# One branch for crowded experts at the end of a two-block transformer kernel, in place of one branch in each expert layer

## The chip, the cores and the metric

One core of one Trainium2 chip runs the whole program. The metric is device time in microseconds (us) of one execution, from three runs of a kernel; beside them one further execution is recorded by the hardware profiler. The program has five instruction streams: TensorE (PE in the profile, with its weight loads as PEld), VectorE (DVE), ScalarE (ACT), GpSimd (POOL) and SyncE (SP). All weight loads are issued from SP's queue.

## What is computed

A sequence of 256 tokens of width 1024 goes through one block (gated feed-forward, a mix of dilated attention and a recurrence, a second feed-forward) and then through a second block with two mixing layers, each followed by a layer of 16 experts. The change touches the expert layers, from here on called layer 0 and layer 1. Cut to what matters, the reference is:

```python
def grouped_moe(x, router_w, router_bias, w1, w3, w2):      # x: 256 tokens, 16 experts of width 512
    ...
    _, idx = lax.top_k(jnp.where(in_group, sel, -jnp.inf), TOP_K)     # 2 experts of one group of 4
    ...
    h = jax.nn.silu(jnp.einsum('td,edf->etf', xt, w1)) * jnp.einsum('td,edf->etf', xt, w3)
    h = h * gates.T[:, :, None].astype(h.dtype)
    y = jnp.einsum('etf,efd->td', h, w2)

for i in range(DEPTH_2):                                     # the second block, 2 layers
    mix = ...                                                # s5 + pooling (i = 0), stick-breaking attention (i = 1)
    x = layer_norm(DEEPNORM_ALPHA * x + mix, ln_mix_g[i], ln_mix_b[i])
    ple = (p[i] @ ple_w_proj[i]) * jax.nn.sigmoid(x @ ple_w_gate[i])
    ffn = grouped_moe(x, router_w, router_bias, moe_w1[i], moe_w3[i], moe_w2[i])
    x = layer_norm(DEEPNORM_ALPHA * x + ffn + ple, ln_ffn_g[i], ln_ffn_b[i])
```

## The kernel before, in words

The kernel gives every expert room for CAP = 64 tokens. `router` (line 1181) chooses the experts, numbers the tokens of each one, and counts: `cn` is the largest number of tokens that any expert got, `ci` the same as an integer. An expert with more than 64 tokens is crowded; the tokens beyond 64 are then computed by `overflow` (line 1504), which sends all 256 tokens through all 16 experts.

`moe_layer` (line 1277) runs the experts in eight pairs, p = 0 to 7. For each pair TensorE does, in a written order (each instruction is chained to the one before by `pinned`, line 337): `combine` of the pair before (tiles `early` for p below 3, `comb` from 3 on), `hidden_T` (tile `ehT`, four transposes) and `slots_T` (tile `ohTp`), the first up-projection of the next pair (tile `h`), the down-projection of this pair (tile `ey`), the gate chunks of the embedding (tile `gacc`, for p up to 3), and the second up-projection of the next pair (tile `h` again; the trace shows its result multiplied on DVE as `es`). An up-projection reads eight weight tiles of 512 KB, a down-projection eight. Two up-projections and one down-projection make 24 tiles a pair.

At p = 4, ahead of everything else of that pair, each layer holds its branch (lines 1460 to 1464):

```python
            if p == 4:
                del cur["pin"]
                v = nc.values_load(ci[0:1, 0:1], min_val=0, max_val=T)
                with tc.If(v > CAP):
                    overflow(i, x, nh, nl, late, row)
                cur["pin"] = None
```

Each of the five engines loads the count into a register (TENSOR_LOAD, line 1461), compares and branches (COMPARE_BRANCH, line 1462), and, where the body is left out, adds to its semaphores what the body would have added (EVENT_SEMAPHORE, line 1462) before it goes on. SP has eight of these, one for each DMA semaphore. Right after the branch comes `residual` (line 1428): it adds the two halves of the layer's transposed input (`whole_h`, `whole_l`) on DVE into four tiles `yT`, transposes them back on TensorE (tile `yn`, 16 transposes of 128x128) and adds the result to the accumulators `acc`. After that stands `combine` for pair 3.

Weights come through class `Stream` (line 251): a list `specs` of all loads in the order of their use, a ring of 11 slots of 512 KB, from line 1652 on 13 more, and at the start of each expert layer some slots lent by other pools. `next` (line 286) hands out the next tile and issues the loads that fit. In SP's queue a load waits until the tile that had its slot has been read, and until the load eight places ahead of it has landed (eight DMA semaphores in turn). The scheduler of the framework orders each engine's instructions within a stretch without branches; the branch of each layer is the end of one such stretch, and nothing moves over it.

`layer_norm_out` (line 1151) ends the program: SP issues four output transfers, waits on all semaphores and the engines meet (line 1749).

Of the kernel before, what the change touches and what calls it, by code (L numbers as in the profile page):

```python
# [15 lines left out]
P = 128  # L16
# [33 lines left out]
def transformer_kernel(ctx: ExitStack, tc: tile.TileContext, A, out, stop=None):  # L50
# [10 lines left out]
    psum = ctx.enter_context(tc.tile_pool(name="ps", bufs=4, space=bass.MemoryType.PSUM))  # L61
    pacc = ctx.enter_context(tc.tile_pool(name="pa", bufs=4, space=bass.MemoryType.PSUM))
# [176 lines left out]

    moe_specs(0)  # L240
# [10 lines left out]
    class Stream:  # L251
# [16 lines left out]
        def ahead(self, n):  # L268
            while self.n < min(len(specs), self.pos + n):
                ap = specs[self.n]  # L270
                t = self.slot([ap.shape[1], ap.shape[2]], f"w{self.n}")
                self.loads.append(nc.sync.dma_start(t, ap))
                self.tiles.append(t)
                self.n += 1

# [45 lines left out]
    def after(i, j):  # L321

        tc.add_manual_dep(i.ins, j.ins.name, mybir.DependencyInfo(
            mybir.DependencyClass.NoSync, mybir.DependencyReason.DATA), reason="order")
# [771 lines left out]
    def layer_norm_T(x, before, row, eps, then=None):  # L1096
# [23 lines left out]
        for i in range(2):  # L1120
            halves = before(i)
            r, m, _ = ln_stats(halves, eps)
            cur["z"] = S.activation(x[i][:, :512], halves[0], AF.Identity, scale=r, bias=m)
            cur["zv"] = V.tensor_scalar(x[i][:, 512:], halves[1], r, m, op0=OP.mult, op1=OP.add)
# [56 lines left out]
    def router(p, parts):  # L1181
# [45 lines left out]
        cn = SM([1], name="cn")  # L1227
        V.tensor_reduce(cn, pk[:, 2, :], axis=AX.X, op=OP.max)
        ci = spool.tile([P, 1], I32, tag="ci", name="ci", bufs=2)
        V.tensor_copy(ci, cn)  # L1230
# [6 lines left out]
        late = SM([2, NE], name="late")  # L1237
        V.tensor_scalar(late, rk, float(CAP), None, op0=OP.is_ge)
        V.scalar_tensor_tensor(late, late, 1.0 / ALPHA, sc, op0=OP.mult, op1=OP.mult)
        return oh, rk, sc, late, ci  # L1240
# [36 lines left out]
    def moe_layer(i, x, before, row, eps, next_gains):  # L1277
# [32 lines left out]
        def then(t, qs):  # L1310
# [6 lines left out]
            elif t == 1:  # L1317
# [8 lines left out]
                G.tensor_tensor(nl[1], x[1], fb(nh[1]), op=OP.subtract)  # L1326
            elif t == 2:
                routed.extend(router(lg, parts))
                W.lend(LEND)
                gather(0, routed[0])  # L1330
                W.lend([H, H])
                W.lend([X,XH]*2, 18)

        xT = layer_norm_T(x, before, row, eps, then)
        oh, rk, sc, late, ci = routed
# [92 lines left out]
        def residual():  # L1428

            for kk in range(2):  # L1430
                yT = [Q([2, T], name="yT") for _ in range(2)]
                for n in range(2):
                    c = slice(2 * n, 2 * n + 2)
                    V.tensor_tensor(yT[n], fb(whole_h[kk])[:, c], fb(whole_l[kk])[:, c], op=OP.add)  # L1434
                for t in range(2):
                    pn = PT([4, P], name="yn")
                    for k in range(4):
                        pinned(PE.transpose(pn[:, k, :], yT[k // 2][:, k % 2, t * P:(t + 1) * P], ident))  # L1438
# [19 lines left out]
        for p in range(8):  # L1458
            if p == 4:
                del cur["pin"]  # L1460
                v = nc.values_load(ci[0:1, 0:1], min_val=0, max_val=T)
                with tc.If(v > CAP):
                    overflow(i, x, nh, nl, late, row)
                cur["pin"] = None
# [9 lines left out]
            if p == last + 1:  # L1474
                residual()
# [18 lines left out]
            if p == last:  # L1494
                embedding()
            if p < 7:
                h3 = PT([512], name="h3")
                up(p + 1, h3)
                s = hidden(h1, h3)
        combine(7, y, o)  # L1500
# [3 lines left out]
    def overflow(i, x, nh, nl, late, row):  # L1504
# [5 lines left out]
        for k in range(8):  # L1510
            p = PT([2, P], name="ofp")
            for t in range(2):
                PE.transpose(p[:, t, :], xf[t][:, k * P:(k + 1) * P], ident)
# [139 lines left out]
    eps = (1e-5, 1e-5 / ALPHA ** 2)  # L1653
    f = moe_layer(0, xt, f, 0, eps[0], (2, 2))
    f = stick(xt, f, 2, eps[1])
    f = moe_layer(1, xt, f, 4, eps[0], (6, 2))
    layer_norm_out(f, eps[1])

# [94 lines left out]
```

## Time and profile before

| | us |
|---|---|
| median of three runs | 1308.74 |
| the three runs | 1304.94, 1308.74, 1309.45 |
| the profiled execution, device time | 1304.89 |
| its span, first to last instruction | 1302.7 |
| TensorE busy in the span | 1241.5 (95%) |
| mean granted TensorE clock | 0.972 of full |

The span is what the views of the trace measure; the device time of the same execution is 2.2 us longer. Layer 0 lies between about 629 and 893 us of the span, layer 1 between about 1023 us and the end. An instruction that ends in "q" in a row (DVEq, SPq) is one of the engine's sequencer: it branches, waits or issues, and does not count as busy. In the trace an up-projection has 32 records of `h`, two for each matmul of the program.

### The profile page before, as it was taken

What the parts mean: (1) busy time and instruction counts of PE and PEld (TensorE: products, weight loads), DVE (VectorE), ACT (ScalarE), POOL (GpSimd) and SP (SyncE); (2) the same over time, 40 slices, a digit from 0 to 9 for tenths busy, and PEclk for the clock granted to TensorE, in tenths of its full rate; (3) what the DMA queues carried; (4) which work ended last, traced back from release to release, by engine and by line L of the source; (5) the groups of instructions that cost most, each with busy time, mean ns of one, the idle gap of its engine ahead of it and who ended that gap; (6) DMA issues with size and microseconds to landing.
All of it is one profiled execution on the core that took longest, in us unless ns stands there. A gap on an engine that the chain in (4) does not pass through costs nothing. (4 is left out here: it accounts for less than half of the span.)

```text
span 1302.7 us, 19644 instructions
## 1 busy us (share of the span) xinstructions
PE 1241.5 (95%) x7726; PEld 906.6 (70%) x7726; DVE 607.7 (47%) x975; ACT 514.9 (40%) x774; POOL 269.3 (21%) x318
## 2 busy tenths in 40 slices
PE   8999999999999999998999997997999999997996
PEld 7999997887898999897635453445988734454433
DVE  6445548886664645477512123115755514114113
ACT  5444445575444554435421131114677422122111
POOL 4000001002499547213101220002311101220001
PEclk9999999999898999999999998998999899998998
DMA  9765565435454556536899997999835698998995
GB/s 342 232 188 184 181 191 178 131 130 169 138 179 128 176 152 199 165 128 229 325 395 384 386 385 276 395 398 369 329 112 180 218 373 302 383 389 311 358 393 216
DMA packets 175273, 335.36 MB, mean 257 GB/s; under 512 B 10337, under 2 KB 72305, under 8 KB 175170
## 3 DMA queue, kind: packets, MB, share of 16 engines
q1 hardware_dynamic: 173696, 330.34, 71.8%
q0 software_dynamic: 896, 2.98, 0.6%
q8 instruction: 64, 1.05, 0.3%
q10 hardware_dynamic: 578, 0.67, 0.2%
q14 instruction: 39, 0.32, 0.1%
HBM read 332.91 MB, written 1.05 MB: 256 GB/s over the span
## 5 line engine op out<-in xcount | busy, mean ns | idle before, releaser
L316 DVE TENSOR_TENSOR wlo<-w,whi 128x1024 fp32r<-128x1024 f32 x200 | 266.2, 1338 | 208.5 <-ACT whi L301 205.8
L301 ACT ACTIVATE whi<-w 128x1024 fp32r<-128x1024 f32 x234 | 246.4, 1059 | 247.3 <-PE hT L346 118.8
L350 PE MATMUL h<-w,xg 128*64 128x512 f32 x1024 | 225.6, 594 | 0.5
L345 PE MATMUL hT<-xTh,whi 128*128 128x256 f32 x704 | 202.1, 287 | 0.1
L346 PE MATMUL hT<-xTl,whi 128*128 128x256 f32 x704 | 201.3, 286 | 0.4 <-DVE xTl L334 0.3
L347 PE MATMUL hT<-xTh,wlo 128*128 128x256 f32 x704 | 200.8, 286 | 0.0
L350 PEld LDWEIGHTS h<-w,xg 128*64 128x64 f32 x1024 | 72.3, 137 | 137.8 <-issue 132.1
L345 PEld LDWEIGHTS hT<-xTh,whi 128*128 128x128 f32 x704 | 137.3, 195 | 1.5 <-ACT xTh L332 0.5
L346 PEld LDWEIGHTS hT<-xTl,whi 128*128 128x128 f32 x704 | 137.1, 195 | 1.4 <-DVE xTl L334 0.8
L347 PEld LDWEIGHTS hT<-xTh,wlo 128*128 128x128 f32 x704 | 136.9, 195 | 0.0
L350 PE MATMUL ey<-w,ehTs 128*64 128x512 f32 x512 | 114.2, 593 | 0.4
L335 DVE SCALAR_TENSOR_TENSOR yl<-ey,sgate,yh 128x512 fp32r<-128x512 f32 x32 | 24.0, 749 | 180.1 <-ACT yh L332 179.0
L332 ACT ACTIVATE yh<-ey,sgate 128x512 fp32r<-128x512 f32 x32 | 22.0, 688 | 167.6 <-PE ey L350 127.3
L350 PEld LDWEIGHTS ey<-w,ehTs 128*64 128x64 f32 x512 | 38.6, 137 | 70.8 <-issue 62.8
L316 POOL TENSOR_TENSOR wlo<-w,whi 128x1024 fp32r<-128x1024 f32 x16 | 37.7, 2382 | 222.2 <-ACT whi L301 142.4
L345 PE MATMUL tr<-xTh,whi 128*128 128x256 f32 x256 | 73.9, 289 | 0.4 <-ACT xTh L332 0.4
L346 PE MATMUL tr<-xTl,whi 128*128 128x256 f32 x256 | 73.2, 286 | 0.3 <-DVE xTl L334 0.3
L347 PE MATMUL tr<-xTh,wlo 128*128 128x256 f32 x256 | 72.6, 284 | 0.0
L346 PE MATMUL yacc<-wlo,hh 128*128 128x512 f32 x176 | 68.7, 391 | 0.0
L345 PE MATMUL yacc<-whi,hh 128*128 128x512 f32 x176 | 68.7, 390 | 0.0
L347 PE MATMUL yacc<-whi,hl 128*128 128x512 f32 x176 | 68.6, 390 | 0.0
L357 POOL TENSOR_TENSOR brs<-rp,cm 128x1 f32<-128x1 f32 x8 | 4.4, 550 | 299.3 <-DVE rp L356 297.4
(444 smaller groups left out, 2138.1 us busy)
## 6 DMA issues: line engine op xcount, KB each, us to landing
w<-in_moe_w SPq DMA_DIRECT2D x384, 512.0 KB, 10.2
w<-in_ffn_w SPq DMA_DIRECT2D x132, 512.0 KB, 4.3
w<-in_w_in SPq DMA_DIRECT2D x28, 512.0 KB, 3.9
w<-in_sb_qkv SPq DMA_DIRECT2D x24, 512.0 KB, 10.5
w<-in_ple_gate SPq DMA_DIRECT2D x16, 512.0 KB, 9.0
w<-in_w_out SPq DMA_DIRECT2D x8, 512.0 KB, 3.2
w<-in_ab_w_in SPq DMA_DIRECT2D x8, 512.0 KB, 4.4
w<-in_ab_w_out SPq DMA_DIRECT2D x8, 512.0 KB, 4.1
```

What stands on the lines that cost most here:

```text
L301: a = S.activation(hi, t, AF.Copy)
L316: i = eng.tensor_tensor(lo, t, fb(hi), op=OP.subtract)
L332: cur["act"] = S.activation(hi, src, AF.Copy if isinstance(scale, float) else AF.Identity, scale=scale)
L335: return V.scalar_tensor_tensor(lo, src, scale, fb(hi), op0=OP.mult, op1=OP.subtract)
L345: pinned(PE.matmul(o, lh, rh, start=start, stop=False))
L346: pinned(PE.matmul(o, lh, rl, start=False, stop=False))
L347: pinned(PE.matmul(o, ll, rh, start=False, stop=stop))
L350: pinned(PE.matmul(o, l, r, start=start, stop=stop, **kw))
L357: cur["pow"] = G.tensor_tensor(o, t, cm05[:, :n], op=OP.pow)
```

## The change

- Both branches inside the layers go, and with them the calls of `overflow` on the path that is always run. `late` (the weights of the tokens beyond 64) is no longer computed there.
- The count of layer 1's router is the maximum of both layers' counts; only then it is made an integer.
- `residual` is issued right after the second up-projection of pair 4, in the body of p = 3, and its sum on DVE is made ahead of `embedding`, as two tiles `whole` of 128x1024 instead of four `yT` of 128x512.
- Two transfers of 512 KB are added in layer 0: the layer's input goes from SBUF to two tiles `kept` in DRAM.
- At the end of the program one branch stands behind `layer_norm_out`. Its body reads `kept` back, sets the weight stream back to the first load of layer 0, and runs layer 0, the attention, layer 1 and the output again, with `overflow` called in both layers.

```diff
...
+    dpool = ctx.enter_context(tc.tile_pool(name="dram", bufs=1, space=bass.MemoryType.DRAM))
...
+    base = len(specs)
     moe_specs(0)
...
+        def back(self, n):
+
+            self.n = self.pos = n
+            del self.tiles[n:]
+            self.lent = {}
+            self.ahead(self.depth())
...
-        for i in range(2):
+        for i in range(2 if before else 0):
             halves = before(i)
...
-        cn = SM([1], name="cn")
+
+        cn = spool.tile([P, 1], F32, tag="cn", name="cn", bufs=2)
         V.tensor_reduce(cn, pk[:, 2, :], axis=AX.X, op=OP.max)
-        ci = spool.tile([P, 1], I32, tag="ci", name="ci", bufs=2)
-        V.tensor_copy(ci, cn)
+        if cur.get("cn") is not None:
+            V.tensor_tensor(cn, cn, cur["cn"], op=OP.max)
+        cur["cn"] = cn
...
-        late = SM([2, NE], name="late")
-        V.tensor_scalar(late, rk, float(CAP), None, op0=OP.is_ge)
-        V.scalar_tensor_tensor(late, late, 1.0 / ALPHA, sc, op0=OP.mult, op1=OP.mult)
-        return oh, rk, sc, late, ci
+        late = None
+        if crowded:
+            late = SM([2, NE], name="late")
+            V.tensor_scalar(late, rk, float(CAP), None, op0=OP.is_ge)
+            V.scalar_tensor_tensor(late, late, 1.0 / ALPHA, sc, op0=OP.mult, op1=OP.mult)
+        return oh, rk, sc, late
...
                 G.tensor_tensor(nl[1], x[1], fb(nh[1]), op=OP.subtract)
+                if i == 0 and not crowded:
+                    for u in range(2):
+                        nc.sync.dma_start(kept[u], x[u])
...
             for kk in range(2):
-                yT = [Q([2, T], name="yT") for _ in range(2)]
-                for n in range(2):
-                    c = slice(2 * n, 2 * n + 2)
-                    V.tensor_tensor(yT[n], fb(whole_h[kk])[:, c], fb(whole_l[kk])[:, c], op=OP.add)
                 for t in range(2):
                     pn = PT([4, P], name="yn")
                     for k in range(4):
-                        pinned(PE.transpose(pn[:, k, :], yT[k // 2][:, k % 2, t * P:(t + 1) * P], ident))
+                        pinned(PE.transpose(pn[:, k, :], whole[kk][:, k, t * P:(t + 1) * P], ident))
...
-            if p == 4:
-                del cur["pin"]
-                v = nc.values_load(ci[0:1, 0:1], min_val=0, max_val=T)
-                with tc.If(v > CAP):
-                    overflow(i, x, nh, nl, late, row)
-                cur["pin"] = None
+            if p == 4 and crowded:
+                overflow(i, x, nh, nl, late, row)
...
             if p == last + 1:
-                residual()
                 comb = [[PA([512], name="comb") for _ in range(2)] for _ in range(2)]
...
             if p == last:
+                whole = [X([4, T], name="whole") for _ in range(2)]
+                for kk in range(2):
+                    V.tensor_tensor(whole[kk], fb(whole_h[kk]), fb(whole_l[kk]), op=OP.add)
                 embedding()
             if p < 7:
                 h3 = PT([512], name="h3")
                 up(p + 1, h3)
                 s = hidden(h1, h3)
+                if p == last:
+                    residual()
...
+    kept = [dpool.tile([P, D], F32, tag=f"kept{u}", name=f"kept{u}") for u in range(2)]
     f = moe_layer(0, xt, f, 0, eps[0], (2, 2))
     f = stick(xt, f, 2, eps[1])
     f = moe_layer(1, xt, f, 4, eps[0], (6, 2))
+    ci = spool.tile([P, 1], I32, tag="ci", name="ci", bufs=1)
+    V.tensor_copy(ci, cur["cn"])
+    v = nc.values_load(ci[0:1, 0:1], min_val=0, max_val=T)
     layer_norm_out(f, eps[1])
+    with tc.If(v > CAP):
...
+        W.back(base)
+        x = [H([D], name="again") for _ in range(2)]
+        for u in range(2):
+            nc.sync.dma_start(x[u], kept[u])
+        f = moe_layer(0, x, None, 0, eps[0], (2, 2), crowded=True)
+        f = stick(x, f, 2, eps[1])
+        f = moe_layer(1, x, f, 4, eps[0], (6, 2), crowded=True)
+        layer_norm_out(f, eps[1])
```

`last` is 3. Where the change puts these instructions shows in the order of the built programs. The first place is TensorE at the branch of layer 0: `h_` is the second up-projection of pair 4, `ofp` and `ofh` belong to the body. Before:

```order
4105 L350 MATMUL h_7666<-w_7532,xg 64x512
4106 L1461 TENSOR_LOAD ci
4107 L1462 COMPARE_AND_BRANCH
4108 L1513 MATMUL ofp<-identr,of 128x128 x16
...
4253 L1462 UNCONDITIONAL_BRANCH x2
4254 L1438 MATMUL yn<-identr,yT 128x128 x16
4255 L350 MATMUL comb<-yh,ohT 128x512
```

And with the change:

```order
4105 L361 MATMUL h_7671<-w_7533,xg 64x512
4106 L1452 MATMUL yn<-identr,whole 128x128 x16
4107 L361 MATMUL comb<-yh,ohT 128x512
4108 L361 MATMUL comb<-yl,ohT 128x512
```

The 16 transposes and the eight `comb` stand where they stood; only the load of the count and the branch between them and `h` are gone. Layer 1 has the same.

The second place is DVE at the same point of layer 0 with the change (`es` is the product of the up-projections, `pg` the embedding's gate):

```order
546 L1269 TENSOR_SCALAR sgate<-ohTp 64x1 x2
547 L1506 TENSOR_TENSOR whole<-xTh,xTl 128x1024
548 L346 SCALAR_TENSOR_TENSOR yl<-ey,sgate,yh 128x512 x2
549 L1506 TENSOR_TENSOR whole<-xTh,xTl 128x1024
550 L1443 TENSOR_TENSOR pg<-pg,pro 128x512 x2
551 L1444 TENSOR_TENSOR acc<-acc,pg 128x512 x2
552 L1443 TENSOR_TENSOR pg<-pg,pro 128x512 x2
553 L1444 TENSOR_TENSOR acc<-acc,pg 128x512 x2
554 L1368 TENSOR_TENSOR es<-es,h_7671 128x512
555 L1454 TENSOR_TENSOR acc<-acc,yn 128x512 x4
```

Before, two `yT` stood ahead of `es` and two more between the additions of `yn`; now both sums are made ahead of the embedding.

The third place is SP at the start of layer 0 with the change, and at the end of the program:

```order
213 L274 DMA w_6752<-in_moe_w 128x2x512
214 L1344 DMA kept_6558<-x_87 128x1024
215 L274 DMA w_6754<-in_moe_w 128x1024
216 L1344 DMA kept_6559<-x_88 128x1024
217 L274 DMA w_6756<-in_moe_w 128x1024
...
221 L274 DMA w_6596<-in_moe_w 128x2x512
222 L274 DMA w_6764<-in_moe_w 128x1024
223 L274 DMA w_6766<-in_moe_w 128x1024
...
634 L1179 DMA out<-o 128x832
635 L1676 COMPARE_AND_BRANCH
```

The two copies stand between weight loads; the load in row 221 (its slot comes free with the tile `pro`) had stood two loads later. SP's branch stands behind the last output transfer, and each other engine's branch behind its last instruction; the body that they pass over has 5183 instructions on TensorE, 920 on DVE, 643 on ACT, 131 on POOL and 1560 on SP.

## Rows read from the trace of the kernel before

**Rows 1.** The page: the span.

```profile
span 1302.7 us, 19644 instructions
```

**Rows 2.** PE around layer 0's branch: start us, us, operation, [idle before <-releaser].

```profile
781.26 7.09 PE L350 MATMUL h<-w,xg 128*64 128x512 f32 x32
795.07 1.94 PE L1438 MATMUL yn<-identr,yT 128*128 128x128 f32 x8 [6.72 <-DVEq L1462]
...
799.94 0.78 PE L350 MATMUL comb<-yh,ohT 128*128 128x512 f32 x1
...
804.50 7.09 PE L350 MATMUL h<-w,xg 128*64 128x512 f32 x32
```

**Rows 3.** The same around layer 1's branch.

```profile
1186.47 0.60 PE L350 MATMUL h<-w,xg 128*64 128x512 f32 x2
1193.69 1.94 PE L1438 MATMUL yn<-identr,yT 128*128 128x128 f32 x8 [6.62 <-DVEq L1462]
...
1203.61 2.79 PE L350 MATMUL h<-w,xg 128*64 128x512 f32 x12
```

**Rows 4.** The same one pair later in layer 0, where no branch stands.

```profile
829.19 0.40 PE L350 MATMUL comb<-yh,ohT 128*128 128x512 f32 x1
...
831.03 0.60 PE L1356 MATMUL ehT<-identr,es 128*128 128x128 f32 x4
831.47 0.38 PE L1246 MATMUL ohTp<-identr,oh 128*128 128x128 f32 x2
...
832.14 2.37 PE L350 MATMUL h<-w,xg 128*64 128x512 f32 x10
```

**Rows 5.** Layer 0's branch by engine: ns min/median/max, first and last start us.

```profile
L1462 ACTq COMPARE_BRANCH  x1: 45/45/45, 783.1 to 783.1; - x1
L1462 ACTq EVENT_SEMAPHORE  x1: 17/17/17, 784.6 to 784.6; - x1
L1462 DVEq COMPARE_BRANCH  x1: 72/72/72, 789.2 to 789.2; - x1
L1462 DVEq EVENT_SEMAPHORE  x1: 21/21/21, 794.9 to 794.9; - x1
```

**Rows 6.** SP's longest wait of layer 0's stretch; SP's branch in layer 1.

```profile
SPq L1462 <- SPq L1462: 9.4, 1, 9.4
L1462 SPq EVENT_SEMAPHORE  x8: 17/17/17, 1171.1 to 1174.2; - x8
L1462 SPq COMPARE_BRANCH  x1: 50/50/50, 1165.7 to 1165.7; - x1
```

**Rows 7.** By stretch: us, busy PE PEld DVE ACT POOL, clock, DMA share, GB/s.

```profile
790.00:820.00 30.00, 23.86 (x106) 12.04 (x108) 8.04 (x13) 4.81 (x7) 0.00 (x0) 0.83 0.74 264
820.00:886.00 66.00, 65.90 (x331) 30.26 (x329) 8.85 (x20) 8.80 (x16) 0.00 (x0) 1.00 1.04 397
1165.00:1223.00 58.00, 49.90 (x226) 24.38 (x224) 17.18 (x27) 11.74 (x16) 0.97 (x1) 0.91 0.87 324
1223.00:1285.00 62.00, 61.90 (x312) 29.06 (x310) 8.19 (x17) 8.80 (x16) 0.00 (x0) 1.00 1.03 394
```

**Rows 8.** A wait at the end of layer 1; PE there, pair 7's down-projection.

```profile
PEld ey L350 <- DMA w<-in_moe_w: 0.8, 2, 0.5
1281.04 7.78 PE L350 MATMUL ey<-w,ehTs 128*64 128x512 f32 x32
```

**Rows 9.** DVE ahead of layer 0's branch.

```profile
784.86 1.29 DVE L1434 TENSOR_TENSOR yT<-xTh,xTl 128x512 f32<-128x512 f32 x2
```

**Rows 10.** ACT where layer 0's input is finished; SP's longest wait there.

```profile
632.42 0.83 ACT L1123 ACTIVATE x<-x,brs 128x512 f32<-128x512 f32 x1
SPq L272 <- PE pro L1268: 10.2, 2, 10.0
```

**Rows 11.** The end: SP's last transfer and its semaphore instructions.

```profile
1299.17 0.33 SPq L1168 DMA_DIRECT2D out<-o  x1
L1749 SPq EVENT_SEMAPHORE  x14: 17/28/28, 1299.6 to 1302.7; - x14
```

More of the change, by code (lines that the diff above doesn't have):

```diff
@@ L321, in after @@
     def after(i, j):
+        if j is None:
+            return
         tc.add_manual_dep(i.ins, j.ins.name, mybir.DependencyInfo(
@@ L1179, in onehot, with router @@
         return oh
-    def router(p, parts):
+    def router(p, parts, crowded):
         sc = SM([2, NE], name="score")
@@ L1275, in ple_projection, with moe_layer @@
         return [part(t, j) for t in range(2) for j in range(2)]
-    def moe_layer(i, x, before, row, eps, next_gains):
+    def moe_layer(i, x, before, row, eps, next_gains, crowded=False):
         pro = [M([D], name="pro") for _ in range(2)]
@@ L1326, in then @@
                 G.tensor_tensor(nl[1], x[1], fb(nh[1]), op=OP.subtract)
+                if i == 0 and not crowded:
+                    for u in range(2):
+                        nc.sync.dma_start(kept[u], x[u])
             elif t == 2:
-                routed.extend(router(lg, parts))
+                routed.extend(router(lg, parts, crowded))
                 W.lend(LEND)
@@ L1334, in moe_layer @@
         xT = layer_norm_T(x, before, row, eps, then)
-        oh, rk, sc, late, ci = routed
+        oh, rk, sc, late = routed
         def up(p, h, chunks=range(4)):
@@ L1512, in overflow @@
             for t in range(2):
-                PE.transpose(p[:, t, :], xf[t][:, k * P:(k + 1) * P], ident)
+                pinned(PE.transpose(p[:, t, :], xf[t][:, k * P:(k + 1) * P], ident))
             S.activation(xT[k // 4][:, k % 4, :], p.rearrange("p a b -> p (a b)"), AF.Identity,
@@ L1656, in transformer_kernel @@
     f = moe_layer(1, xt, f, 4, eps[0], (6, 2))
+    ci = spool.tile([P, 1], I32, tag="ci", name="ci", bufs=1)
+    V.tensor_copy(ci, cur["cn"])
+    v = nc.values_load(ci[0:1, 0:1], min_val=0, max_val=T)
     layer_norm_out(f, eps[1])
+    with tc.If(v > CAP):
+        for n in [n for n in cur if n != "both"]:
+            del cur[n]
+        cur.update({n: None for n in ("z", "zv", "hold")})
+        W.back(base)
[6 more added lines that the diff above has]
+        layer_norm_out(f, eps[1])
 def _constants():
```

## The prediction

> **What bounds the kernel now.** The span is 1302.7 us [rows 1]. I read TensorE's timeline first, at the two places where a branch stands. In layer 0 the second up-projection of pair 4 ends at 781.26 + 7.09 = 788.35; nothing runs on TensorE for 6.72 us, until an instruction of the branch on DVE lets it go; then come 16 transposes, the eight `comb` from 799.94 on, and the next up-projection only at 804.50 [rows 2]. From up-projection to up-projection that is 16.15 us. In layer 1 it goes from 1187.07 (1186.47 + 0.60) to 1203.61, 16.54 us [rows 3]. One pair later, without a branch and without transposes, the same `comb`, `ehT` and `ohTp` take 832.14 - 829.19 = 2.95 us, and four transposes 831.47 - 831.03 = 0.44 [rows 4]. These two places are the only wide gaps that TensorE has in the two layers.
>
> Why the gap is that long is told by the sequencers' rows. DVE's COMPARE_BRANCH takes 72 ns at 789.2, but its next instruction comes at 794.9, 5.7 us later [rows 5]; TensorE's first transpose waits for just that one. SP needs longer still: 9.4 us in layer 0, and in layer 1 5.4 us (1165.7 to 1171.1) to the first of its eight semaphore instructions [rows 6]. While SP stands there, no weights are requested.
>
> So the third view is the traffic by stretch. After layer 0's branch the DMA engines move 397 GB/s until the layer's end; in the 30 us around the gap only 264 [rows 7]. The missing part is (397 - 264) / 397 x 30 = 10.1 us of transfer. Around layer 1's branch it is (394 - 324) / 394 x 58 = 10.3 us [rows 7]. This matters since the weights are as scarce as TensorE: at the end of layer 1 TensorE waits for loads, and the last down-projection takes 7.78 us [rows 8] where an up-projection of as many records takes 7.09 [rows 2].
>
> **The change part by part.** *Both branches go.* What is left for TensorE between the up-projections is 16 transposes, at the pace of rows 4 16 / 4 x 0.44 = 1.76 us (an estimate, at full clock), and the 2.95 us of rows 4: 4.71. Freed are 16.15 - 4.71 = 11.44 us in layer 0 and 16.54 - 4.71 = 11.83 in layer 1, 23.3 in all. Part of it is the clock: the granted clock is 0.83 and 0.91 of full in the stretches around the branches and 1.00 in those behind them [rows 7], because TensorE fell to its lower level when it stood idle. The transposes' own needs are met: their sums are made ahead of the embedding, three of the four `yn` tiles take banks that were read long before, and the fourth follows `es`, which is done while the first twelve transposes run.
>
> *What is late next* are the weights. TensorE would arrive 11.4 and 11.8 us earlier at the end of the layers, but at their ends it waits for loads already, so it can gain there only what the loads gain. They can gain what they lost, 10.1 and 10.3 us: SP is no longer held, and the slots come free earlier since TensorE reads earlier. So I count 20.4 us and not 23.3. Ends for this term: nothing from below (the loads come no earlier at all), 23.3 from above. I take 20.4 since the queue's standstill is a row of its own and no load is missing a slot because of anything that stays.
>
> *The sums* `whole` cover the same columns as four `yT` (two of them take 1.29 us [rows 9]), so they cost DVE the same 2.6 us a layer; they move ahead of the embedding, where DVE waits for the gate chunks. The second has to wait for a slot that a gate chunk's low half leaves. Cost 0; without that cover at most 2.6 a layer, a bound that I don't count. The two `late` instructions and the copy of the count, all small, leave the router in layer 0; in layer 1 a maximum comes in. Cost 0, they stand behind what TensorE waits for.
>
> *The two copies to DRAM* are 0.52 MB each, 1.3 us apiece at 397 GB/s, 2.6 in all. The second waits in SP's queue until layer 0's input is finished on ACT at 632.42 + 0.83 = 633.25 [rows 10], and holds all loads behind it. But SP stands still there anyway, 10.0 us for the tile `pro` [rows 10], and the load that waits for `pro` now stands two loads earlier. I take 0, because the layer's first tiles are requested far ahead and the queue has several short stops in the pairs that follow; 2.6 is the upper end.
>
> *The branch at the end.* SP's last transfer is issued at 1299.17 + 0.33 = 1299.5, its closing semaphores run from 1299.6 to 1302.7 [rows 11]. Now a jump lies between. For its price the nearest rows are SP's own: 5.4 and 9.4 us [rows 6]. The other engines' jumps start with their last instruction, ahead of SP's last transfer, so SP's decides. Behind it come the eight semaphore instructions and the closing ones, without the wait for the last transfer, which has landed by then: between 0 and the 3.1 us of rows 11; I take 2.2, since the meeting of the engines stays as it is. The end is then 1299.5 + 5.4 + 2.2 = 1307.1 to 1299.5 + 9.4 + 2.2 = 1311.1, that is 4.4 to 8.4 us more. I take the middle, 6.4.
>
> Advanced Engine Details and Errata in the Trainium skill, section Control Flow Timing, puts a compare-and-branch at about 108 ns. The instruction alone agrees (45 and 72 ns in rows 5), the time until the engine's next one does not; by the page's figure the end would cost 0.1 us for the jump and the sum would be a gain of 20 us.
>
> **The sum** is -20.4 + 6.4 = -14.0 us. The profiled execution took 1304.89, so 1290.9. The median of the runs shown, 1308.74, lies 3.85 above it; of the four executions two are at 1304.9 and two at 1308.7 to 1309.5. I add half of the distance, 1.9: 1292.8.
>
> **The rivals.** *A short jump at the end.* ACT passed its branch in 1.5 us (783.1 to 784.6 [rows 5]), over a short body and with work of its own to wait for; and at the end no weights are in flight. With 1.5 the end is 1299.5 + 1.5 + 2.2 = 1303.2, 0.5 more than before, and the sum -19.9: 1286.9. Against it: 5.4 and 5.7 us came on two engines and in both layers, nearly alike, which looks like a fixed delay and not like traffic. The page's figure of 108 ns points this way.
>
> *Jumps that queue.* SP's 9.4 us came 1.9 us behind DVE's branch, its 5.4 with none close ahead; were the difference, 4.0, the price of each engine ahead, three (ACT, POOL, DVE) would make it 5.4 + 12 = 17.4, the end 16.4 later, and the sum -4.0: 1302.8, about no change. Against it: DVE's own 5.7 came behind TensorE's branch and was not longer. Runtime: NRT & Kernel Launch in the Trainium skill, section Instruction fetch mechanics, says that a branch past the two pages held has to fetch its target by DMA; over the large body at the end that would hold for ACT and POOL too.
>
> *Half of the loads' time comes back.* If slots and not SP's standstill held the loads, perhaps half of the 20.4 is gained: -10.2 + 6.4 = -3.8, 1303.0, no change.
>
> *Slower: the weights set the end and come no earlier.* TensorE then waits in pairs 5 to 7 for what it gained, both layers end where they ended, and the new end is paid on top: +6.4, 1313.2, with the upper price 1315. The place is the last two pairs of each layer; it turns slower than before when less than 6.4 of the 20.4 us come back. For it: the loads' wait in rows 8. Against it: in the 30 us around layer 0's branch a third of the traffic is missing, and what held it is removed.
>
> *The branch at the end is taken.* Then two layers and the attention run again. Both branches were passed over before, and the count is the larger of the same two, so I give it next to nothing.
>
> **How the numbers follow.** No change is within 0.5%, 6.5 us, about what a measurement of this kernel can tell. The forecast has 0.68, the short jump 0.13, half of the loads' time 0.07, queuing jumps 0.06, the slower case 0.05, the taken branch 0.01. Faster is the forecast and the short jump, 0.81; the same 0.13; slower 0.06. The range goes down to the short jump at the profiled execution's level (1304.89 - 19.9 = 1285.0, less one) and up to the forecast with its worst ends at the median's level: 1308.74 - 20.4 + 8.4 + 2.6 = 1299.3, and a little more for loads that come back in part: 1284 to 1301.
>
> **What would show it.** Right: between the up-projections around the 16 `yn` TensorE has no idle row, the clock stays at 1.00, the stretch takes about 4.7 us; the traffic does not fall below 380 GB/s there; the last down-projection of each layer is longer than 7.78 and waits for loads by one to three us in pairs 6 and 7. At the end SP shows a COMPARE_BRANCH and 5 to 9 us until its next instruction. Wrong: a wait of `yn` for DVE, a traffic gap that stays, waits of pair 0 or 1 for weights behind `kept`, or an end that comes within 2 us of the last transfer's landing, or more than 10 after it.

## The result, and the profile after

The changed kernel took 1289.65 us (median of four runs, 1284.18 to 1291.71), the kernel before 1308.38 (four runs); the ratio is 0.9867, with a 95% interval from 0.9844 to 0.9890. The profiled execution took 1288.41 us, 16.5 less than that of before (1304.89); the prediction had 14.0 less. The medians lie 18.7 us apart here, and 15.4 and 13.2 in two later measurements of the same two kernels (given below beside other runs); the prediction's 1292.8 was 15.9 below its median. The page's span:

```profile
span 1286.7 us, 19601 instructions
```

TensorE's timeline of the changed kernel around the two places where the branches stood (start us, us, operation):

```profile
781.07 7.09 PE L361 MATMUL h<-w,xg 128*64 128x512 f32 x32
788.08 1.97 PE L1452 MATMUL yn<-identr,whole 128*128 128x128 f32 x16
789.80 0.48 PE L361 MATMUL comb<-yh,ohT 128*128 128x512 f32 x1
...
792.83 7.09 PE L361 MATMUL h<-w,xg 128*64 128x512 f32 x32
...
1172.18 7.09 PE L361 MATMUL h<-w,xg 128*64 128x512 f32 x32
1179.20 1.97 PE L1452 MATMUL yn<-identr,whole 128*128 128x128 f32 x16
...
1183.94 7.09 PE L361 MATMUL h<-w,xg 128*64 128x512 f32 x32
```

They answer to [rows 2, 3]. From the transposes to the next up-projection it is 4.75 and 4.74 us, with no idle row in either place. The traffic and the clock in the stretches that answer to [rows 7] (us, busy PE PEld DVE ACT POOL, clock, DMA share, GB/s):

```profile
784.00:812.00 28.00, 28.00 (x144) 12.00 (x142) 8.58 (x15) 4.96 (x8) 0.00 (x0) 1.00 1.05 392
812.00:878.00 66.00, 65.33 (x318) 30.02 (x316) 8.23 (x18) 9.57 (x18) 0.00 (x0) 1.00 1.04 396
1158.00:1215.00 57.00, 57.00 (x292) 29.42 (x290) 18.72 (x31) 14.71 (x22) 0.66 (x1) 1.00 1.04 395
1215.00:1271.00 56.00, 55.64 (x257) 23.08 (x254) 5.75 (x11) 6.79 (x12) 0.00 (x0) 1.00 0.96 367
```

The holes of 264 and 324 GB/s are gone, and the clock is at full speed throughout. What is given back shows at the end of each layer, in TensorE's timeline of the last up- and down-projection:

```profile
858.05 4.79 PE L361 MATMUL h<-w,xg 128*64 128x512 f32 x18
863.12 2.42 PE L361 MATMUL h<-w,xg 128*64 128x512 f32 x8 [0.28 <-DMA w<-in_moe_w]
865.82 1.93 PE L361 MATMUL h<-w,xg 128*64 128x512 f32 x6 [0.28 <-DMA w<-in_moe_w]
...
872.78 7.79 PE L361 MATMUL ey<-w,ehTs 128*64 128x512 f32 x32
...
1249.16 6.28 PE L361 MATMUL h<-w,xg 128*64 128x512 f32 x26
1255.69 1.93 PE L361 MATMUL h<-w,xg 128*64 128x512 f32 x6 [0.26 <-DMA w<-in_moe_w]
```

Only small idle pieces are marked, but the last up-projection takes 865.82 + 1.93 - 858.05 = 9.70 us in layer 0 and 8.46 in layer 1, where one that waits for nothing takes 7.09. Most of the rest stands with the weight loads ahead of the matmuls (PEld, 857 to 868 us):

```profile
PEld h L361 <- DMA w<-in_moe_w: 3.7, 6, 1.2
```

To see where the 16.0 us of span went, the program is cut at landmarks. A *stretch* runs, in each layer, from the start of pair 4's second up-projection (781.07 and 1172.18 above) to the first `comb` behind the layer's last down-projection. All in us, from the timelines; *next* is the time from the stretch's start to the next up-projection:

| kernel | start | layer 0: next, stretch | between | layer 1: next, stretch | last matmul to the span's end |
|---|---|---|---|---|---|
| before | 781.26 | 23.24, 108.19 | 290.53 | 23.63, 108.76 | 10.84 |
| after | 781.07 | 11.76, 99.44 | 291.68 | 11.76, 98.19 | 13.20 |
| difference | -0.2 | -8.75 | +1.15 | -10.57 | +2.4 |

So the two stretches gave 19.3 us, the part between them took 1.15 back, and the new end 2.4. The end of the changed kernel, in the rows of the branch's line (ns min/median/max, first and last start us) and in SP's waits from 1270 us on (us, times, longest):

```profile
L1676 SPq EVENT_SEMAPHORE  x8: 17/17/17, 1284.5 to 1285.0; - x8
L1676 PEldq COMPARE_BRANCH  x1: 3620/3620/3620, 1273.1 to 1273.1; - x1
L1676 POOLq COMPARE_BRANCH  x1: 53/53/53, 1280.0 to 1280.0; - x1
L1676 DVEq COMPARE_BRANCH  x1: 76/76/76, 1280.2 to 1280.2; - x1
L1676 POOLq EVENT_SEMAPHORE  x1: 17/17/17, 1280.5 to 1280.5; - x1
L1676 SPq COMPARE_BRANCH  x1: 45/45/45, 1281.2 to 1281.2; - x1
L1676 DVEq EVENT_SEMAPHORE  x1: 21/21/21, 1283.2 to 1283.2; - x1
```

```profile
SPq L1676 <- SPq L1676: 3.3, 1, 3.3
```

A *jump* is the time from an engine's COMPARE_BRANCH to its next instruction. SP's takes 3.3 us (1281.2 to 1284.5), not 5.4 or 9.4 as in [rows 6], TensorE's 3.6, DVE's 3.0 and POOL's 0.5.

### The profile page after: what moved, and what is told of

Read it like the earlier page. It is cut to its first block, busy times and chain, and to the rows that moved or that the text cites. A ratio compares the mean times of both kernels' runs of the same rounds, so it can differ in the third digit from the quotient of the medians.

```text
span 1286.7 us, 19601 instructions
## 1 busy us (share of the span) xinstructions
PE 1237.8 (96%) x7726; PEld 901.8 (70%) x7726; DVE 606.5 (47%) x967; ACT 514.2 (40%) x774; POOL 270.0 (21%) x318
## 4 chain that ended last, share of the span: by engine, by line
PE 64%; issue 14%; POOL 7%; DMA 6%; DVE 5%; ACT 3%; ACTq 0%; POOLq 0%; DVEq 0%; SPq 0%
PE h L361 14%; PE ey L361 7%; DMA w<-in_moe_w 5%; PE xgp L361 3%; PE hT L356 2%; PE hT L357 2%; PE hT L358 2%; PE tr L357 2%; PE tr L356 2%; PE tr L358 2%; PE oacc L358 2%; PE oacc L356 2%; PE nat L356 2%; PE nat L357 2%; PE nat L358 2%
## 5 line engine op out<-in xcount | busy, mean ns | idle before, releaser
L361 PE MATMUL h<-w,xg 128*64 128x512 f32 x1024 | 228.8, 595 | 1.3 <-DMA w<-in_moe_w 0.8
L1368 DVE TENSOR_TENSOR es<-es,h 128x512 f32<-128x512 f32 x16 | 11.0, 687 | 119.0 <-PE h L361 105.6
## 6 DMA issues: line engine op xcount, KB each, us to landing
w<-in_moe_w SPq DMA_DIRECT2D x384, 512.0 KB, 10.3
w<-in_sb_qkv SPq DMA_DIRECT2D x24, 512.0 KB, 10.3
```

Of the source, the lines that this page charges most:

```text
L361: pinned(PE.matmul(o, l, r, start=start, stop=stop, **kw))
L1368: V.tensor_tensor(s, s, h3, op=OP.mult)
```

## The experiments

The question is not whether the branches cost what they seemed to, but by what: by holding SP's queue, as the prediction has it, or by holding TensorE, which then frees no slots. SP's waits bear on both. In the 40 us of layer 1 around the place, before and then after:

```profile
SPq L272 <- PE h L350: 14.0, 4, 11.6
```

```profile
SPq L274 <- PE h L361: 9.9, 8, 3.7
```

Behind its own jump, SP waited 11.6 us in one piece for the up-projection that TensorE began only after the gap. In layer 0 its jump, 9.4 us, fell into the gap itself, and its longest wait for an up-projection behind that was 4.6. The first two experiments separate the two holds. All are edits of the changed kernel, with no branch in the layers.

### pe_hold: TensorE held, SP free

```diff
-            V.tensor_tensor(s, s, h3, op=OP.mult)
+            cur["es"] = V.tensor_tensor(s, s, h3, op=OP.mult)
...
-                for kk in range(2):
-                    V.tensor_tensor(whole[kk], fb(whole_h[kk]), fb(whole_l[kk]), op=OP.add)
+                V.tensor_tensor(whole[1], fb(whole_h[1]), fb(whole_l[1]), op=OP.add)
                 embedding()
...
                 if p == last:
+                    for _ in range(5):
+                        j = V.tensor_tensor(whole[0], fb(whole_h[0]), fb(whole_l[0]), op=OP.add)
+                        after(j, cur["es"])
                     residual()
```

> The changed kernel with one of the two sums written five times, after the product es, so that TensorE has to stand still ahead of its 16 transposes in both layers while SP is free: es ends at 788.99 us in the changed kernel, five sums of 1.23 us end at 795.1, and TensorE idles for about 7.0 us per layer (it did for 6.7 with the branch). Theory SLOTS (the loads' lost time is TensorE's: slots come free only when it reads): in the changed kernel SP waits for a slot from 791.63 to 794.79 us; now until about 801.8, the first tile lands about 4 us later than in the changed kernel or more, and each layer ends 4 to 7 us later: 1298 to 1304 us. Theory QUEUE (the loads lost SP's own standstill, as the prediction has it): no more than 1 us per layer, 1290 to 1292 us.

1303.24 us, ratio 0.9989 (0.9975 to 1.0003): nearly all of the gain is gone. TensorE's row in layer 0, and SP's waits for up-projections from 781 to 815 us and from 1172 to 1212:

```profile
795.21 3.64 PE L1452 MATMUL yn<-identr,whole 128*128 128x128 f32 x16 [7.15 <-DVE whole L1513]
```

```profile
SPq L274 <- PE h L361: 15.7, 6, 11.9
...
SPq L274 <- PE h L361: 17.6, 7, 12.6
```

TensorE stands for 7.15 us, and SP, which no branch holds, stands 11.9 and 12.6 us for the slot that the next up-projection frees. The granted clock is 0.68 of full in the 6.85 us behind the standstill and 1.00 again from the next up-projection on. QUEUE, which gave 1290 to 1292, is ruled out, and the time is the one that SLOTS gave. Whether it is the loads' lag that sets the layers' ends, as SLOTS has it, or TensorE's own delay, the table below tells.

### sp_hold: SP held, TensorE free

```diff
                 h3 = PT([512], name="h3")
+                if p == last and not crowded:
+                    tc.add_manual_dep(W.loads[(317, 551)[i]].ins, cur["pin"].ins.name, mybir.DependencyInfo(
+                        mybir.DependencyClass.Sync, mybir.DependencyReason.DATA), reason="hold")
                 up(p + 1, h3)
```

> The changed kernel with one load of pair 4 in each layer made to wait for the last gate chunk's matmul on TensorE: SP stands still for about 9.1 us in layer 0 (772.0 to 781.1) and 9.7 in layer 1, as it did for its jump, and TensorE's order and waits stay. Theory QUEUE: each layer ends about 9 us later, 1306 to 1309 us. Theory SLOTS: eight loads are under way when SP stops, which keeps the DMA engines busy for about 10 us; 1 to 3 us per layer are lost, 1292 to 1296 us.

1295.13 us, ratio 0.9923 (0.9894 to 0.9952). SP's waits for that matmul in the two layers:

```profile
SPq L274 <- PE gacc L358: 10.5, 1, 10.5
...
SPq L274 <- PE gacc L358: 9.8, 1, 9.8
```

A standstill of 10 us (the branch held SP for 9.4 in layer 0 and 5.4 in layer 1) makes the stretches of the profiled execution 3.9 and 4.3 us longer (103.36 and 102.51). That execution, at 1298.54 us, is the longest of the four; the median lies inside the 1292 to 1296 of SLOTS. QUEUE wanted 9 a layer and is ruled out. The hold stands ahead of the up-projection, as the jump of layer 1 did; that of layer 0 came behind it, from 791.1 us on.

### late_sums: how short a wait of TensorE is free

```diff
-                for kk in range(2):
-                    V.tensor_tensor(whole[kk], fb(whole_h[kk]), fb(whole_l[kk]), op=OP.add)
                 embedding()
...
                 if p == last:
+                    for kk in range(2):
+                        after(V.tensor_tensor(whole[kk], fb(whole_h[kk]), fb(whole_l[kk]), op=OP.add), cur["es"])
                     residual()
```

`cur["es"]` is the product's instruction, as in pe_hold.

> The changed kernel with both sums back behind the product es, where DVE made them before: TensorE waits for them about 2.2 us and then about 0.5 us again, 2.7 us per layer. If TensorE's own time were what counts: 5.4 us, 1295 us. If the loads set the layers' ends (both SLOTS and QUEUE): a wait this short is within what is under way on the DMA engines, 0 to 1 us per layer, 1290 to 1292 us.

1290.84 us, ratio 0.9889 (0.9858 to 0.9919), not to be told from the changed kernel. TensorE waits 2.11 us in each layer; the next up-projection comes 2.4 and 3.8 us later, and the stretches are 98.98 and 99.85 long: 0.5 less and 1.7 more. Three profiles of the changed kernel lie 1.5 apart in layer 1 (98.19, 98.23, 99.74), so a wait of this size costs little or nothing, and no cost shows for where DVE makes the sums.

### both_holds: does SP's standstill count beside TensorE's?

The edits of pe_hold and sp_hold together.

> The changed kernel with both holds at once: SP stands still for about 9 us ahead of the second up-projection of pair 4, as in the one kernel, and TensorE for about 7 us behind it, as in the other; no branch stands in the layers. Alone, SP's hold made the last combine come 8.5 us later than in the changed kernel, TensorE's 11.9 us. Theory SUM (each standstill costs its own transfers): 20 us later, about 1.004 of the kernel before. Theory LARGER (TensorE's standstill lets the loads catch up on what SP's cost, so that the loads' lag at the end is TensorE's delay less 2 to 3 us, whatever SP lost before): 11 to 13 us later, as with TensorE's hold alone, 0.998 to 1.000 of the kernel before; then SP's jump cost the kernel before next to nothing.

1303.61 us, ratio 0.9983 (0.9969 to 0.9997): the time is that of LARGER, and SUM is ruled out. The six kernels side by side, from their timelines:

| kernel | layer 0: next, stretch, rest | layer 1: next, stretch, rest |
|---|---|---|
| before | 23.24, 108.19, 84.95 | 23.63, 108.76, 85.13 |
| pe_hold | 21.09, 105.38, 84.29 | 21.07, 105.32, 84.25 |
| both_holds | 21.54, 106.00, 84.46 | 21.20, 105.82, 84.62 |
| late_sums | 14.19, 98.98, 84.79 | 15.60, 99.85, 84.25 |
| after | 11.76, 99.44, 87.68 | 11.76, 98.19, 86.43 |
| sp_hold | 11.77, 103.36, 91.59 | 11.77, 102.51, 90.74 |

The *rest* is the stretch less *next*. Wherever TensorE was held, it is 84.3 to 85.1 us: TensorE's own work, with next to no wait for loads (in pe_hold the last up- and down-projection of layer 0 take 7.04 and 7.12 us). Where it was not held the rest is longer, since TensorE catches up with the loads and waits: by some 1.3 to 3.4 us in the changed kernel, by 6 to 7 with SP held. SP's hold beside TensorE's adds only 0.5 to 0.6 to a stretch. So in pe_hold, as in the kernel before, the loads were not what set the layers' ends; TensorE's own gap was; SP's jump lay in the shadow of that gap. The kernel before is still 2.2 and 2.9 us a stretch longer than both_holds; 1.7 and 2.4 of that is its longer *next*.

### no_end: the price of the branch at the end

```diff
     f = moe_layer(1, xt, f, 4, eps[0], (6, 2))
-    ci = spool.tile([P, 1], I32, tag="ci", name="ci", bufs=1)
-    V.tensor_copy(ci, cur["cn"])
-    v = nc.values_load(ci[0:1, 0:1], min_val=0, max_val=T)
     layer_norm_out(f, eps[1])
-    with tc.If(v > CAP):
-        ...
```

> The changed kernel without the branch at the end and its body; the copies to DRAM stay, and crowded experts are not redone. The end then has the form of the kernel before: the last transfer issued at 1280.79 us in the changed kernel's trace would be followed by 2.4 us until it has landed and 1.1 us of closing, so the span ends 3.5 us behind that issue and not 5.9: 2.4 us less, about 1287 us. If the branch cost what the prediction gave it: 6.4 us less, 1283 us. If the large body also slows what stands ahead of it, the two layers' ends come earlier too, by any amount.

1288.67 us, ratio 0.9873 (0.9843 to 0.9902), which the runs can't tell from the changed kernel (below: 0.9883 and 0.9888). The trace can: from the last matmul to the span's end it is 10.69 us, and 13.20 in three profiles of the changed kernel (13.20, 13.19, 13.20). The branch costs 2.5 us (2.0 against the end of no_end_no_kept, below, which takes 11.19), and the wait for the last transfers is back in SP's rows:

```profile
SPq L1764 <- DMA out<-o: 1.6, 3, 1.0
```

The stretches (99.74 and 98.26) are those of the changed kernel: the large body slows nothing ahead of it.

### end_traffic and end_small: what makes a jump dear

```diff
-                nc.sync.dma_start(out[i * P:(i + 1) * P, c], o[i][:, c])
+                cur["sent"] = nc.sync.dma_start(out[i * P:(i + 1) * P, c], o[i][:, c])
...
     layer_norm_out(f, eps[1])
+    for n in range(8):
+        t = W.slot([specs[base + 24 + n].shape[1], specs[base + 24 + n].shape[2]], f"again{n}")
+        after(nc.sync.dma_start(t, specs[base + 24 + n]), cur["sent"])
     with tc.If(v > CAP):
```

> The changed kernel with eight loads of 512 KB, whose data nobody reads, issued on SP between the last output transfer and the branch at the end. Theory TRAFFIC (an engine's jump fetches its instructions through the same DMA engines, and waits behind what is under way there): SP's COMPARE_BRANCH to its next instruction, 3.3 us in the changed kernel, becomes 5 us or more, as with the loads of the layers (5.4 and 9.4). Theory PLACE (the jump at the end is shorter by what is jumped over or by where the program stands): it stays at about 3.3 us. The time grows in either case by the eight transfers, about 10 us less what the jump hid, so it says nothing by itself.

With eight loads under way SP's jump takes 1289.0 to 1294.3, 5.2 us:

```profile
L1679 SPq EVENT_SEMAPHORE  x8: 17/17/17, 1294.3 to 1298.8; - x8
...
L1679 SPq COMPARE_BRANCH  x1: 45/45/45, 1289.0 to 1289.0; - x1
```

TRAFFIC's 5 us or more came, in this one profile. The time, 1302.2 us in one run, holds the eight transfers. The other edit keeps the branch and cuts its body:

```diff
     with tc.If(v > CAP):
-        ...
+        layer_norm_out(f, eps[1])
```

> The changed kernel with only the last normalisation and the output's transfers in the body at the end (about 20 instructions per engine in place of hundreds to thousands); crowded experts are not redone. Theory DISTANCE (a jump is dear where its target is far, near targets cost little, as POOL's 0.5 us in the changed kernel): SP's jump falls from 3.3 us to under 1, those of ACT (2.5), DVE (3.0) and TensorE (3.6) too, and the end again waits for the last transfer's landing. Theory FLAT (every jump costs a fetch): they stay within 0.5 us of these.

```profile
L1676 SPq EVENT_SEMAPHORE  x4: 17/17/17, 1282.3 to 1282.6; - x4
L1676 PEldq COMPARE_BRANCH  x1: 363/363/363, 1274.1 to 1274.1; - x1
...
L1676 DVEq COMPARE_BRANCH  x1: 76/76/76, 1281.1 to 1281.1; - x1
...
L1676 DVEq EVENT_SEMAPHORE  x1: 21/21/21, 1281.8 to 1281.8; - x1
L1676 SPq COMPARE_BRANCH  x1: 50/50/50, 1282.1 to 1282.1; - x1
```

SP's jump takes 0.2 us in place of 3.3, DVE's 0.6 for 3.0 (0.63 before the rows are rounded), TensorE's 0.4 for 3.6; the end is 10.67 us long, as without any branch (10.69). DISTANCE holds: all of the 2.5 us is the length of what is jumped over. The trace also counts the DMA packets that bring instructions. From TensorE's branch to 1285.1 us there are ten in the changed kernel and two in end_small:

```profile
q14 instruction: 8, 0.07, 2.1%
q8 instruction: 2, 0.03, 1.1%
...
q8 instruction: 1, 0.02, 0.5%
q14 instruction: 1, 0.01, 0.2%
```

The last of them before SP goes on, taken for SP's own, starts 1.8 us behind SP's branch in the changed kernel and 3.6 behind it in end_traffic, and from there SP needs 1.5 and 1.6 us more: what the traffic lengthens is the time until the packet comes. The Trainium skill, in "Runtime: NRT & Kernel Launch", section Instruction fetch mechanics, says that a taken branch out of the two pages held must fetch its target by DMA; these two runs agree. They add the price: 3.3 us on SP with the DMA engines nearly idle, 5.2 with eight loads under way.

### no_end_no_kept: the price of the copies

no_end, and in addition:

```diff
-                if i == 0 and not crowded:
-                    for u in range(2):
-                        nc.sync.dma_start(kept[u], x[u])
```

> The changed kernel without the branch at the end and without the two copies of layer 0's input to DRAM; crowded experts are not redone. In the changed kernel's trace the loads of layer 0 land 2.3 us later than before from 684 to 720 us, 1.4 later at 735, 0.7 later at 771: the copies' transfer time, worked off in part. If the copies cost what the prediction took, 0: the time of the kernel without the end branch, with which it shares the rest. If what is left of the lag at 771 us goes through to the layer's end, as the other lags did: 0.7 to 1 us less. Upper bound of the prediction: 2.6 us less.

1285.26 us, ratio 0.9847 (0.9832 to 0.9863). The changed kernel itself ran beside it as yardstick:

> The changed kernel itself once more, as the yardstick for the runs beside it: both theories expect the ratio of its first measurement, 0.987 of the kernel before.

It took 1290.03 us, ratio 0.9883 (0.9868 to 0.9899). End branch and copies together cost 0.0036 of 1305 us, 4.7 us; with 2.5 for the end, 2.2 are left for the copies. The two intervals leave some 3 us of room either way, so the split rests on the traces: without the copies layer 0's stretch is 98.34 us long, 1.1 less than after's 99.44, and the part between the stretches 290.74, 0.9 less than 291.68 (against no_end's 99.74 and 292.24 it is 1.4 and 1.5 less); layer 1's stretch is unchanged (98.42). What the copies did shows in SP's waits from 618 to 645 us, first in the changed kernel, then without the copies:

```profile
SPq L1344 <- DVE x L1135: 8.6, 2, 5.5
SPq L274 <- PE pro L1283: 7.1, 1, 7.1
...
SPq L274 <- PE pro L1283: 11.5, 1, 11.5
```

SP does not stand longer: all its waits in these 27 us sum to 18.9 us with the copies and to 19.0 without, and the load that waits for `pro` goes out at 642.8 and 642.5 us. But by then, counted in the traces, SP has issued 216 weight loads with the copies and 218 without, as in the kernel before. Two loads of 512 KB, 1.3 us each at 392 GB/s, have moved behind that wait.

### other_queue: the same program with less on SP

```diff
-                        nc.sync.dma_start(kept[u], x[u])
+                        nc.scalar.dma_start(kept[u], x[u])
...
-                nc.sync.dma_start(out[i * P:(i + 1) * P, c], o[i][:, c])
-            nc.sync.dma_start(out[i * P:(i + 1) * P, SPLIT:], o[i][:, SPLIT:])
+                nc.scalar.dma_start(out[i * P:(i + 1) * P, c], o[i][:, c])
+            nc.scalar.dma_start(out[i * P:(i + 1) * P, SPLIT:], o[i][:, SPLIT:])
```

> The changed kernel with the two copies to DRAM and the output's four transfers issued on ACT's queue in place of SP's. In the changed kernel SP waits for layer 0's input behind the copies (5.5 us to 628.5 and 3.1 us to 632.8), with loads queued behind them; without the copies at all, layer 0 ended 1.5 us earlier and the rest 2.1. If that cost is SP's hold and not the copies' transfer: 1.5 to 2 us come back, and w210's load stands where it stood before. At the end SP jumps while the last work is done, and ACT's jump (2.5 us in the changed kernel, SP's 3.3) comes last: about 1 us less. Together 2 to 3 us less than the changed kernel beside it, 0.986 of the kernel before. If the copies' transfer time is what costs: 1 us less.

> The changed kernel itself, as the yardstick beside the others: 0.988 of the kernel before, as in its last measurement.

1287.36 us, ratio 0.9861 (0.9835 to 0.9886), beside 1290.88, ratio 0.9888 (0.9868 to 0.9908): the intervals overlap, so that it is better is not shown. Its one profile has the two parts that were expected: the end is 12.04 us long, 1.2 less, and layer 0's stretch and the part between are those without copies (98.54 and 290.76), though the copies are still transferred: SP has issued 220 weight loads there when it waits for `pro`. But the stretch starts at 785.90 us, 3.3 to 4.8 later than in the three profiles of the changed kernel; against the first of them, 2.6 of the 4.8 arise between 407 and 644 us, up to where ACT now issues the copies among its own operations. Whether that belongs to the edit or to the one execution stays open. It does show another long jump, in the shadow of the last loads: SP branches at 1262.3 and goes on at 1269.6.

```profile
L1676 SPq EVENT_SEMAPHORE  x8: 17/17/17, 1269.6 to 1287.5; - x8
L1676 SPq COMPARE_BRANCH  x1: 45/45/45, 1262.3 to 1262.3; - x1
```

### spread: a version meant to be faster, and slower

TensorE now waits for loads at each layer's end; the gate chunks of the embedding could fill those waits.

```diff
-PLE = (0, 0, 0, 2, 5, 8)
+PLE = (0, 0, 0, 2, 4, 6, 8)
```

> The changed kernel with the eight gate chunks of each layer spread over pairs 1 to 4 (two each) in place of pairs 1 to 3 (two, three, three); the embedding and the residual move on by one pair. TensorE waits for loads at the end of each layer: the last up-projection takes 9.6 us from start to end in layer 0 and 8.4 in layer 1 where another takes 6.9, and the last down-projection 7.8 in place of 6.9, 6.0 us in all. With two chunks (5.4 us of TensorE) behind pair 3, TensorE reads the tiles of pairs 1 to 3 earlier and slots come free earlier. If slots limit the loads there: up to 6 us less, 1281 us at the level of the first measurement. If the DMA engines have no room to take more there (they move 392 GB/s from 644 to 772 us and 375 from 1085 to 1163, of 397 at most, which leaves 1.6 and 4.3 us): 1 to 4 us less, mostly in layer 1. If neither counts: no change.

1300.36 us, ratio 0.9954 (0.9939 to 0.9968): slower than the changed kernel by 10 us, which none of the three cases had. At pair 4's chunks in layer 0, and the same in layer 1, TensorE waits for their halves:

```profile
PE gacc L357 <- POOL wlo L325: 2.7, 1, 2.7
PE gacc L356 <- ACT whi L310: 1.8, 1, 1.8
```

ACT makes the chunk's high half only behind the two `yh` of the pair's down-projection, and POOL the low half behind that, so nothing is ready when TensorE comes to the chunk. These 4.5 us a layer are TensorE's largest new wait; that they make up the loss is not shown, since the profiled execution is 15.6 us longer than that of the changed kernel and the traffic is lower in it as well (375 GB/s in place of 392 from 644 to 772 us). The idea itself was not tried with the halves made early.

## Why the prediction was right, and which step was not

**The freed time.** The prediction counted 4.71 us from the transposes to the next up-projection; it is 4.75 and 4.74, at full clock. TensorE's way from up-projection to up-projection became 11.5 and 11.9 us shorter (23.24 and 23.63 less 11.76), as counted.

**The 20.4 us.** The size held, the reason did not. The two stretches gave 19.3 us, and 20.2 without the copies (108.19 - 98.34 and 108.76 - 98.42). The step that failed is "I take 20.4 since the queue's standstill is a row of its own and no load is missing a slot because of anything that stays". SP's standstill was a row of its own, but it cost nothing of its own: SP held alone costs some 4 us a layer, SP held beside TensorE 0.5. The loads stopped since TensorE stopped reading. The row that says so, SP's 11.6 us for the up-projection behind the gap, was there to be read and was not (nor was SP's 5.4 us in layer 1 longer than DVE's jump there, 5.9). The right account is the other one: TensorE frees 23.4 us and waits anew for loads, 4.0 us (2.7 and 1.3, from the rests 87.68 and 86.43 against 84.95 and 85.13). Both accounts end near 20 because TensorE, freed, catches up with the loads and then goes at their pace: what is gained is the transfer that was missing around the gap, 10.1 and 10.3 us by the prediction, whatever had stopped it (9.85 and 10.34 without the copies). So the size did not depend on the wrong step and is no evidence for it.

**The copies**, set at 0, cost about 2 us, inside the upper end of 2.6. That "SP stands still there anyway" was right. What failed is to put at nothing that "the load that waits for `pro` now stands two loads earlier": two weight loads fewer were issued ahead of that wait, the loads landed 2.3 us later at 684 us, and with 392 GB/s moved from 644 us on there was little room to make that up before the layer's end.

**The end**, set at 6.4 us, is 2.4: the mis-sized term. The 2.2 us behind the jump held (1284.5 to 1286.7). The jump itself was priced from rows in which loads were under way. The prediction saw this ("at the end no weights are in flight") and put it with the rival of the short jump; 3.3 us lies between that rival's 1.5 and the forecast's 5.4. Its argument against that rival, that 5.4 and 5.7 us look like a fixed delay and not like traffic, failed: SP's jump over the same body takes 3.3 us at the quiet end and 5.2 with eight loads under way (end_traffic). The 1.5 us of ACT that it leaned on came over a short body, and by end_small a jump over a short body is cheap anyway. By the prediction's own way of adding, a jump of 0.1 us would have ended the kernel 0.9 us earlier than before, a gain of 21.3 and not of 20.

**The sum** was -20.4 + 6.4 = -14.0; it came out as -19.3 + 1.15 + 2.4 - 0.2 = -16.0 in the span, or, with the copies apart, as some -20.2 + 2 + 2.4 - 0.2. The copies were set 2 us too low and the end 4 too high; that these two errors partly cancelled was luck.

**The rivals.** Queuing jumps: SP's was the last of five and took 3.3 us, no more than TensorE's 3.6, which was the first. Half of the loads' time, and loads that come no earlier: both are ruled out by the stretches, though TensorE's new waits are their weak form. The branch was not taken.

**The signs** named in the prediction. Of those for right came: no idle row, clock 1.00, 4.7 us and traffic above 380 GB/s at both places, as said. The waits for loads came in the last up-projection (9.70 and 8.46 us) more than in the last down-projection (7.79 and 7.83, about the 7.78 of [rows 8]). So a longer last down-projection did not come, nor did the 5 to 9 us of SP's jump. Of those for wrong none came: TensorE waits for no load from 644 to 700 us, and the span ends some 3.5 us behind the landing of the last transfer.

## To carry to other kernels

When two engines stop together, look at what each waits for *after* the stop: here the queue's own standstill was the more visible one, but in layer 1 the queue then waited longer still for a slot that the stopped TensorE had not freed. A hold put back on one engine at a time, and then on both, tells which counts; the two did not add up. In these runs a branch whose body is left out cost by how far it jumped and by what the DMA engines carried meanwhile, so one far jump at the quiet end was cheaper than a jump in the middle of a stream of loads. The two copies cost by the loads that they moved behind the queue's next wait; the queue stood no longer for them.

## What the runs showed of the hardware that was not expected

- A compare-and-branch over a short body took 0.2 us on SP, 0.4 on TensorE and 0.6 on DVE to the next instruction (end_small); over the large body 3.3, 3.6 (5.0 in one of three profiles of the changed kernel) and 3.0 with little traffic; with loads under way SP took 5.2 (end_traffic) and 7.3 (other_queue). The Trainium skill's 108 ns ("Advanced Engine Details and Errata", Control Flow Timing) is of the order of the near jump alone; the instruction itself took 45 to 76 ns on SP, ACT, POOL and DVE.
- SP may stand still for 10 us with eight loads of 512 KB under way and cost some 4 us a layer in the profile, not 10 (sp_hold).
- After 7.15 us of idle time the 16 transposes took 3.64 us in place of 1.97 (pe_hold; granted clock 0.68 from 795.21 to 802.06 us), so here a standstill of TensorE costs more than its own length: the next up-projection came 9.3 us later.
- Executions of the same changed kernel differ by up to 1.5 us in where the first matmul of pair 4's up-projection starts (781.07, 781.29, 782.59 us) and in layer 1's stretch; parts of a trace are better compared from a landmark close by than from the start.
